# A two-layer hybrid block on one core: which raw buffer a condition block takes, and at which ticks condition sums are made

## The chip, the cores and the metric

The kernel runs on 1 core of one Trainium2 chip. The metric is the device time of one execution in microseconds (us); it was 1853.11 us as the median of three runs (1845.4 to 1854.9).

The engines of the core, by the names of the profile: PE is the tensor engine (matmuls; PEld its weight loads), DVE the vector engine (VectorE), ACT the scalar engine, POOL the GpSimd engine, SP the engine that issues most transfers (DMAs). Each engine takes its own instructions in program order; semaphores order them across engines.

## The reference

Two layers of a transformer-like block on 512 tokens of width 1024. What matters here is the conditioning vector c: per layer it gives six vectors of 1024 numbers, by a matrix of 1024 x 6144.

```python
c_act = jax.nn.silu(c)
for l in range(DEPTH):                       # DEPTH = 2
    x = hybrid_layer(x, c_act, ...)

def hybrid_layer(x, c_act, ...):
    mod = c_act @ w_ada + b_ada
    shift1, scale1, gate1, shift2, scale2, gate2 = jnp.split(mod, 6, axis=-1)
    h = modulate(rms_norm(x, norm1_g), shift1, scale1)
    ...                                      # projections, three branches, gates
    mixed = jnp.sum(gates * y_br, axis=2) @ w_o
    x = x + gate1[:, None, :] * mixed
    h2 = modulate(rms_norm(x, norm2_g), shift2, scale2)
    u, g = jnp.split(h2 @ w_up, 2, axis=-1)
    u = causal_dwconv(u, w_conv, b_conv)
    y = (jax.nn.silu(u) * g) @ w_down        # D_FF = 2816
    x = x + gate2[:, None, :] * y
    return x
```

## The kernel before

**Weight units.** All large weights are cut into units of 128 x 1024 floats (512 KB), eight blocks of 128 x 128, in the order in which they are used. A unit passes four stations. `dma_to` loads it into one of six raw buffers (`wr`, `NR = 6`; L180, issued by SP). `prep_hi` rounds it on ACT to the matmul's format (`wh`, L194). `prep_lo` takes the remainder on DVE (`wl`, L203); after that the raw buffer is no longer needed. Then PE uses both: `mm3` makes three matmuls for each block (L321 to L323: high times high, high times low, low times high). `wh` and `wl` have five buffers each, and the preparation runs up to four units ahead of use (`depth`).

**Condition blocks.** The six vectors of a layer are 48 columns of 128 numbers, called by section 0 to 5 (shift1, scale1, gate1, shift2, scale2, gate2), eight blocks each. A block is 128 x 1024 floats of `wada`. `ada_dma` loads the next block into a raw buffer of the same six (tile `ar`, L225, issued by SP), one at a time. `ada_sum` multiplies it on DVE by the broadcast condition and sums each row (L230, 128 x 1024 in one instruction, and a read of the accumulator). `ada_step` does the sum of the block that is loaded and at once issues the load of the next. `ada_need(l, sec)` repeats steps until a section is complete. Sections 0 and 1 of layer 0 are made apart at the start; the other 80 blocks go through this queue, in order, layer 0 first.

**Which raw buffer.** The planner `buffer` runs while the program is built. `held[b]` is the number of the unit with which buffer b comes free; a buffer may be taken when `held[b] < state["lo"]`, where `state["lo"]` counts the remainders made so far. Of those it takes the one with the lowest number, that is, the one longest free. A loaded condition block has the number 1 << 30; its sum sets it back.

**When.** The program is written by hand in one order (`manual_schedule`), and each engine takes its part of it. `tick` is called at fixed places between matmuls. It moves small attention work on, runs what is pending (`flush`, such as the evacuation of a finished bank), and calls `ada_step` at every other tick, or at every tick while `ada_fast` is set; `ada_on` switches this on and off. It is on in the mix (gates, branches and the output projection), in the first part of the feed-forward stage and in the down projection.

**Around the change.** The stages of a layer: projections and branches; the mix, whose last tiles `mixed` are split into `mxh` and `mxl` (L562, L563) for the output projection with `w_o`; the feed-forward stage, at first by column blocks, with up to six units loaded ahead, then in three groups of seven half-size products (`ff_group`), for which raw weights are added up in place by accumulating loads from POOL (L186); then the down projection. This has 22 row blocks (kc) for each of 8 column blocks (j). Columns 0 to 2 are computed together, kc by kc, with a tick after every second kc. Columns 3 to 7 follow one by one, with a tick after every fourth kc; in layer 0 column 7 is computed last in two halves, with the next norm (L376 is its first matmul) between. `dn_evac` adds a finished column to x (L1023) and, in layer 0, its square to `acc` (L360, L361). In the down projection `ada_on` and `ada_fast` are set at kc = 8 of the first three columns.

Of the kernel before, what the change touches and what calls it, by code (L numbers as in the profile page):

```python
# [91 lines left out]
def tile_hybrid_layers(ctx: ExitStack, tc: tile.TileContext, xT, cvec, wall, wada, par, a2, cst, tabs, out):  # L92
# [15 lines left out]
    def slot(nm, dt=F32):  # L108
        return slots.tile([128, S], dt, tag="slot", name=nm)

    def bm(nm="bm"):
        return psm.tile([128, S], F32, tag="m", name=nm)
# [32 lines left out]
    state = {"prep": 0, "lo": 0, "dma": 0}  # L145
# [14 lines left out]
    held = [-1] * NR  # L160
# [54 lines left out]
    ada_buf = [0]  # L215
# [10 lines left out]
            ada_raw.append((l, b, post, r))  # L226

    def ada_sum(l, b, r):
        held[ada_buf[0]] = -1
        V.scalar_tensor_tensor(out=r, in0=r, scalar=1.0, in1=cact, op0=ALU.mult, op1=ALU.mult,  # L230
                               accum_out=mod[l][:, b:b + 1])

    def ada_step():
        if ada_raw:
            l, b, post, r = ada_raw.pop(0)
            ada_sum(l, b, r)
            if post:
                post()
        ada_dma()

    def ada_need(l, sec):
        while any(j[:2] <= (l, sec * 8 + 7) for j in ada_raw + ada_jobs):
            ada_step()
# [30 lines left out]
    def flush():  # L274
        while pend:
            pend.pop(0)()

    def advance(kind):
        for g in list(active):
            t = g[1]  # L280
            if g[2] or t[0] != kind:
                continue
            if kind == "p" and live[0] + t[1] > NA:
                return
            if len(t) > 2 and not all(t[2]()):
                return
            g[2] = True
            g[1] = next(g[0], None)
            if g[1] is None:
                active.remove(g)  # L290

    def tick(n=1, fl=True):
        for g in active:
            g[2] = False
        if cool[0] > 0:
            cool[0] -= 1
        if queue and len(active) < 8 and cool[0] == 0:
            it, cool[0] = queue.pop(0)
            active.append([it, next(it), False])
        advance("e")  # L300
        if fl:
            flush()
        advance("p")
        if ada_on[0] and (ada_fast[0] or tickcount[0] % 2 == 1):
            ada_step()
        tickcount[0] += 1
        if DBG:
            print("T", tickcount[0], len(active), len(queue), live[0], cur[0], [g[0].__name__ for g in active])

    tickcount = [0]  # L310
    cool = [0]
    ada_on = [True]
    ada_fast = [False]

    def drain():
        flush()
        while active or queue:
            tick(1)

    def mm3(o, wh, wl, ah, al, first, last):  # L320
        T.matmul(o, lhsT=wh, rhs=ah, start=first, stop=False)  # L321
        T.matmul(o, lhsT=wh, rhs=al, start=False, stop=False)  # L322
        T.matmul(o, lhsT=wl, rhs=ah, start=False, stop=last)  # L323
# [16 lines left out]
    def col_block(act, evac, half=True, ticks=1):  # L340
        ahead()
        wh, wl = unit()
        o = bm()
        for kc in range(KD):
            sl = slice(kc * 128, kc * 128 + 128)
            mm3(o, wh[:, sl], wl[:, sl], act[kc][0], act[kc][1], kc == 0, kc == KD - 1)
            if kc == 3:
                tick(ticks)
        pend.append(lambda: evac(o))
        tick(ticks, False)  # L350
# [204 lines left out]
    def split(src, nm, scale=None):  # L555
        hi = slot(nm + "h", F32R)
        lo = slot(nm + "l", F32R)
        if scale is None:
            A.copy(hi, src)
            V.tensor_tensor(lo, src, hi.bitcast(F32), op=ALU.subtract)  # L560
        else:
            A.activation(hi, src, AF.Copy, scale=scale)  # L562
            V.scalar_tensor_tensor(out=lo, in0=src, scalar=scale, in1=hi.bitcast(F32), op0=ALU.mult, op1=ALU.subtract)  # L563
        return hi, lo

    def layer(l, nm, h):
# [520 lines left out]
        def act_to(n):  # L1087
            for k in range(min(n, KFF)):
                if acts[k] is None:
                    acts[k] = split(act[k], "fa")  # L1090
                    act[k] = None
# [165 lines left out]
        while ada_raw:  # L1257
            i, b, post, r = ada_raw.pop(0)
            ada_sum(i, b, r)
            if post:  # L1260
                post()
# [20 lines left out]
        def wd(j, kc):  # L1282
            f = DNI[j, kc]
            if f // 8 not in got:
                ahead()
                got[f // 8] = unit()
            sl = slice((f % 8) * 128, (f % 8) * 128 + 128)
            return got[f // 8][0][:, sl], got[f // 8][1][:, sl]
# [4 lines left out]
        def dn_evac(j, o):  # L1293
            upd5(j, o)
            if last:
                store(j)
            else:
                square_acc(j, acc3)

        xl = list(range(KD))  # L1300
        act_to(4)
        far[0] = 4
        o2 = [bm() for _ in range(NI)]
        for kc in range(KFF):
            for j in range(NI):
                wh, wl = wd(j, kc)
                mm3(o2[j], wh, wl, acts[kc][0], acts[kc][1], kc == 0, kc == KFF - 1)
            for _ in range(2):
                if rest:
                    rest.pop(0)()  # L1310
            act_to(kc + 4)
            if xl and kc >= 4:
                k = xl.pop(0)
                x[k] = slot("x")
                Q.dma_start(out=x[k], in_=xm[l, k])
            if kc == 8:
                ada_on[0] = True
                ada_fast[0] = True
                far[0] = 1
            if kc % 2:  # L1320
                tick()
        ada_need(l, 5)
        for j in range(NI):
            pend.append(lambda j=j: dn_evac(j, o2[j]))
        for j in range(NI, KD if last else KD - 1):
            o = bm()
            for kc in range(KFF):
                wh, wl = wd(j, kc)
                mm3(o, wh, wl, acts[kc][0], acts[kc][1], kc == 0, kc == KFF - 1)
                if kc % 4 == 3:  # L1330
                    tick()

            pend.append(lambda j=j, o=o: dn_evac(j, o))
        flush()
        ada_fast[0] = False
        if last:
            return None, None
        ada_need(l + 1, 0)
# [5 lines left out]
    with tc.manual_schedule():  # L1344
# [39 lines left out]
        for l in range(L):  # L1384
            nm, h = layer(l, nm, h)
# [171 lines left out]
```

## Time and profile before

| | |
|---|---|
| three runs | 1845.4, 1853.11, 1854.9 us; median 1853.11 |
| the profiled execution | 1846.68 us, its span (first to last instruction) 1844.5 us |
| mean granted TensorE clock | 0.985 |
| ACT busy | 743.5 us (40%) |
| POOL busy | 147.7 us (8%) |
| read from HBM, written | 250.00 MB, 8.40 MB |
| condition blocks loaded by L225 | 80 of 512 KB, first sum at 292.6 us, last at 1262.0 us |
| share of the chain that ended last: PE, DVE, DMA | 72%, 12%, 8% |

How to read the views. A row of groups has line, engine, operation, output <- inputs by the program's tile names, the shape and the count. A row of waits has the waiting engine, tile and line, then the releasing engine, tile and line, then us in total, how many times, and the longest. A row of windows has the window, then for PE, PEld, DVE, ACT and POOL the busy us with the count of instructions, then the granted clock, the share of the 16 DMA engines that was busy, and GB/s. A row of the timeline has start, duration, engine, line, operation; in brackets the idle time of that engine before it and what ended it; SPq is SP's queue of transfers. A row of a tile has minimum, median and maximum duration in ns, then first and last start. The busy time of a matmul overlaps with the next, so a busy PE is not PE at its peak; the distance of starts tells more.

### The profile page before, as it was taken

The page shows a single profiled execution, that of the slowest core. Times are in us where ns is not written, and L with a number is a line of the kernel's source. Part 1 is how long each engine was busy: PE and PEld are TensorE (multiplying, and loading weights), DVE is VectorE, ACT ScalarE, POOL GpSimd, SP SyncE. Part 2 cuts the span into 40 slices and gives each one's busy share as a digit, 9 for nine tenths or more (in the row PEclk, how much of TensorE's full clock was granted, in tenths as well). Part 3 has the DMA queues.
Part 4 walks back from the last instruction along what each step waited for, and adds up shares of the span by engine and source line. Part 5 has one row for each costly group of instructions (what it writes and reads, how often), then busy time and mean ns, then how long its engine had stood idle before and what let it go on. Part 6 is the DMA issues. An engine that isn't in the chain of part 4 may idle for free.

```text
span 1844.5 us, 24358 instructions
## 1 busy us (share of the span) xinstructions
PE 1784.8 (97%) x9601; PEld 1527.7 (83%) x9601; DVE 1085.7 (59%) x1639; ACT 743.5 (40%) x1233; POOL 147.7 (8%) x191
## 2 busy tenths in 40 slices
PE   8999999999899979999869999999999999999999
PEld 6888788888788869998668888788888898899887
DVE  7767654555566766685445667554434466566831
ACT  4664433422234335562115744333323234455520
POOL 3211100000010011100000101000000000111000
PEclk9999999999999989999979999999999999999999
DMA  9331232454462468854453322314242333488421
GB/s 359 126 130 58 74 99 83 146 181 177 168 223 97 161 184 215 212 200 166 177 194 110 108 92 69 104 69 149 92 147 93 122 108 92 121 210 217 160 99 50
DMA packets 78510, 259.99 MB, mean 141 GB/s; under 512 B 9096, under 2 KB 9522, under 8 KB 78396
## 3 DMA queue, kind: packets, MB, share of 16 engines
q1 hardware_dynamic: 68748, 224.86, 34.9%
q0 software_dynamic: 9648, 33.58, 8.6%
q8 instruction: 75, 1.23, 0.3%
q14 instruction: 39, 0.32, 0.0%
HBM read 250.00 MB, written 8.40 MB: 140 GB/s over the span
## 4 chain that ended last, share of the span: by engine, by line
PE 72%; DVE 12%; DMA 8%; ACT 4%; issue 3%; SPq 0%; POOL 0%; DVEq 0%; ACTq 0%; POOLq 0%
PE bm L321 13%; PE bm L322 13%; PE bm L323 13%; DMA ar<-wada 6%; PE bm L460 4%; PE ga L460 4%; PE bm L628 3%; PE bm L629 3%; PE bm L630 3%; PE bm L1159 3%; PE bm L1162 3%; PE bm L1161 3%; DMA wr<-wall 3%; DVE ar L230 2%; DVE wl L203 2%
## 5 line engine op out<-in xcount | busy, mean ns | idle before, releaser
L203 DVE TENSOR_TENSOR wl<-wr,wh 128x1024 fp32r<-128x1024 f32 x338 | 412.4, 1223 | 291.2 <-ACT wh L194 288.1
L194 ACT CAST wh<-wr 128x1024 fp32r<-128x1024 f32 x338 | 351.5, 1047 | 363.2 <-DMA wr<-wall 210.6
L321 PE MATMUL bm<-hhi,wh 128*128 128x512 f32 x912 | 366.1, 401 | 0.0
L323 PE MATMUL bm<-hhi,wl 128*128 128x512 f32 x912 | 355.7, 390 | 0.0
L322 PE MATMUL bm<-hlo,wh 128*128 128x512 f32 x912 | 355.5, 390 | 0.0
L321 PEld LDWEIGHTS bm<-hhi,wh 128*128 128x128 f32 x912 | 171.3, 188 | 37.1 <-issue 2.8
L323 PEld LDWEIGHTS bm<-hhi,wl 128*128 128x128 f32 x912 | 171.2, 188 | 37.1
L322 PEld LDWEIGHTS bm<-hlo,wh 128*128 128x128 f32 x912 | 171.5, 188 | 35.8 <-issue 1.4
L323 PE MATMUL bm<-fah,wl 128*128 128x512 f32 (+1 forms) x374 | 145.9, 390 | 17.2 <-DVE wl L203 17.2
L230 DVE SCALAR_TENSOR_TENSOR ar<-ar,cact 128x1024 f32<-128x1024 f32 x80 | 97.8, 1222 | 91.9 <-DMA ar<-wada 91.8
L321 PE MATMUL bm<-fah,wh 128*128 128x512 f32 (+1 forms) x374 | 145.7, 390 | 1.1 <-ACT wh L194 1.1
L322 PE MATMUL bm<-fal,wh 128*128 128x512 f32 (+1 forms) x374 | 144.9, 387 | 0.0
L323 PEld LDWEIGHTS bm<-fah,wl 128*128 128x128 f32 x374 | 74.5, 199 | 31.9 <-DVE wl L203 18.8
L628 PE MATMUL bm<-wh,hhi 128*128 128x512 f32 (+1 forms) x256 | 96.1, 376 | 0.0
L629 PE MATMUL bm<-wl,hhi 128*128 128x512 f32 (+1 forms) x256 | 93.5, 365 | 0.0
L630 PE MATMUL bm<-wh,hlo 128*128 128x512 f32 (+1 forms) x256 | 93.3, 365 | 0.0
L321 PEld LDWEIGHTS bm<-fah,wh 128*128 128x128 f32 x374 | 74.6, 200 | 14.3 <-ACT wh L194 1.4
L322 PEld LDWEIGHTS bm<-fal,wh 128*128 128x128 f32 x374 | 74.5, 199 | 13.1
L186 POOL DMA_DIRECT2D wr<-wall x48 | 41.7, 987 | 377.3 <-DVE wl L203 215.2
L321 PE MATMUL bm<-mxh,wh 128*128 128x256 f32 (+1 forms) x176 | 59.8, 340 | 8.0 <-ACT mxh L562 8.0
L322 PE MATMUL bm<-mxl,wh 128*128 128x256 f32 (+1 forms) x176 | 59.6, 338 | 0.0
L323 PE MATMUL bm<-mxh,wl 128*128 128x256 f32 (+1 forms) x176 | 59.1, 336 | 0.0
(288 smaller groups left out, 3368.5 us busy)
## 6 DMA issues: line engine op xcount, KB each, us to landing
wr<-wall SPq DMA_DIRECT2D x302, 512.0 KB, 4.3
ar<-wada SPq DMA_DIRECT2D x80, 512.0 KB, 3.5
wr<-wall POOLq DMA_DIRECT2D x48, 512.0 KB, 9.2
ad<-wada SPq DMA_DIRECT2D x32, 256.0 KB, 6.4
x<-xT SPq DMA_DIRECT2D x16, 256.0 KB, 4.5
x<-xm SPq DMA_DIRECT2D x16, 256.0 KB, 5.9
xm<-x POOLq DMA_DIRECT2D x10, 256.0 KB, 2.5
cumb<-cumd POOLq DMA_DIRECT2D x8, 256.0 KB, 4.8
```

Source lines behind the costliest of these rows:

```text
L194: A.copy(hi, raw[plan[i][1]])
L203: V.tensor_tensor(lo, raw[plan[i][1]], hi.bitcast(F32), op=ALU.subtract)
L230: V.scalar_tensor_tensor(out=r, in0=r, scalar=1.0, in1=cact, op0=ALU.mult, op1=ALU.mult, accum_out=mod[l][:, b:b + 1])
L321: T.matmul(o, lhsT=wh, rhs=ah, start=first, stop=False)
L322: T.matmul(o, lhsT=wh, rhs=al, start=False, stop=False)
L323: T.matmul(o, lhsT=wl, rhs=ah, start=False, stop=last)
L460: T.matmul(banks[f % GB][:, ts], lhsT=got[f // 8][wi][:, (f % 8) * 128:(f % 8) * 128 + 128], rhs=h[kc][hi][:, ts], start=kc == 0 and hf != ...
L628: T.matmul(o, lhsT=h[k][0][:, bs], rhs=wh[:, ws], start=k == 0, stop=False)
L629: T.matmul(o, lhsT=h[k][0][:, bs], rhs=wl[:, ws], start=False, stop=False)
L630: T.matmul(o, lhsT=h[k][1][:, bs], rhs=wh[:, ws], start=False, stop=k == KD - 1)
L1159: T.matmul(o, lhsT=wh[:, sl], rhs=ah, start=first and i == 0 and k == 0, stop=False, skip_group_check=True)
L1161: T.matmul(o, lhsT=wh[:, sl], rhs=al, start=False, stop=False, skip_group_check=True)
```

## The change

There are two edits. First, a raw buffer whose sum has been made gets the number `state["lo"] - 1` in place of -1: it still counts as free, but as freed just now, so the planner takes a buffer that has been free for longer. Second, `ada_fast` is removed, so sums are made at every other tick everywhere; in the down projection they begin after the first three columns, ticks in columns 3 and on come after every third kc in place of every fourth, and the call that needs section 5 stands ahead of the stage. Blocks left over stay in the queue for the next layer's mix.

```diff
     def ada_sum(l, b, r):
-        held[ada_buf[0]] = -1
+        held[ada_buf[0]] = state["lo"] - 1
...
-        if ada_on[0] and (ada_fast[0] or tickcount[0] % 2 == 1):
+        if ada_on[0] and tickcount[0] % 2 == 1:
             ada_step()
...
-    ada_fast = [False]
...
         xl = list(range(KD))
+        ada_need(l, 5)
         act_to(4)
...
             if kc == 8:
-                ada_on[0] = True
-                ada_fast[0] = True
                 far[0] = 1
             if kc % 2:
                 tick()
-        ada_need(l, 5)
+        ada_on[0] = True
         for j in range(NI):
             pend.append(lambda j=j: dn_evac(j, o2[j]))
...
-                if kc % 4 == 3:
+                if kc % 3 == 2:
                     tick()
...
         flush()
-        ada_fast[0] = False
```

From L314 up to the head of the down projection, lines of the changed kernel have a number lower by one (L1023 is L1022, L1010 is L1009, L361 is L360). Three places show how instructions move; the buffers that are taken do not show in such rows.

On DVE in the down projection of layer 0, from the update of column 2 on (L1023 or L1022 adds a column to x, L361 or L360 its square; L230 is a sum, L203 the remainder of a weight unit; L252 adds the bias of a section). Before:

```order
670 L1023 SCALAR_TENSOR_TENSOR x<-bm,mod_87,x 128x512
671 L361 TENSOR_TENSOR acc<-acc,sq 128x512
672 L230 SCALAR_TENSOR_TENSOR ar,mod_88<-ar,cact 128x1024
673 L252 TENSOR_TENSOR mod_88<-mod_88,par_86 128x8
674 L203 TENSOR_TENSOR wl<-wr,wh 128x1024
675 L230 SCALAR_TENSOR_TENSOR ar,mod_88<-ar,cact 128x1024 x2
676 L203 TENSOR_TENSOR wl<-wr,wh 128x1024
677 L230 SCALAR_TENSOR_TENSOR ar,mod_88<-ar,cact 128x1024 x2
678 L203 TENSOR_TENSOR wl<-wr,wh 128x1024
679 L1023 SCALAR_TENSOR_TENSOR x<-bm,mod_87,x 128x512
```

And of the change, from a remainder to the update of column 4:

```order
666 L203 TENSOR_TENSOR wl<-wr,wh 128x1024
667 L230 SCALAR_TENSOR_TENSOR ar,mod_88<-ar,cact 128x1024 x2
668 L203 TENSOR_TENSOR wl<-wr,wh 128x1024
669 L1022 SCALAR_TENSOR_TENSOR x<-bm,mod_87,x 128x512
670 L360 TENSOR_TENSOR acc<-acc,sq 128x512
671 L230 SCALAR_TENSOR_TENSOR ar,mod_88<-ar,cact 128x1024
672 L203 TENSOR_TENSOR wl<-wr,wh 128x1024
673 L230 SCALAR_TENSOR_TENSOR ar,mod_88<-ar,cact 128x1024
674 L203 TENSOR_TENSOR wl<-wr,wh 128x1024
675 L230 SCALAR_TENSOR_TENSOR ar,mod_88<-ar,cact 128x1024
676 L203 TENSOR_TENSOR wl<-wr,wh 128x1024
677 L1022 SCALAR_TENSOR_TENSOR x<-bm,mod_87,x 128x512
```

Two sums stood for each remainder at most places; now it is one, or two at some. The stage has 13 sums in place of 26.

On SP at the same stage (L225 loads a condition block, L180 a weight unit). Before:

```order
130 L225 DMA ar<-wada 128x1024 x4
131 L180 DMA wr<-wall 128x1024
132 L225 DMA ar<-wada 128x1024
133 L180 DMA wr<-wall 128x1024
134 L225 DMA ar<-wada 128x1024 x2
135 L180 DMA wr<-wall 128x1024
136 L225 DMA ar<-wada 128x1024 x2
```

And of the change:

```order
128 L180 DMA wr<-wall 128x1024 x2
129 L225 DMA ar<-wada 128x1024
130 L180 DMA wr<-wall 128x1024
131 L225 DMA ar<-wada 128x1024
132 L180 DMA wr<-wall 128x1024
133 L225 DMA ar<-wada 128x1024 x2
134 L180 DMA wr<-wall 128x1024
```

Where one or two (once four) condition loads stood ahead of each weight load, mostly one does.

On DVE in the mix of layer 1 (L1009 and L1010, or L1008 and L1009, are the gated sums of the branches). Before:

```order
1003 L1009 SCALAR_TENSOR_TENSOR mg<-mg,bm 128x512
1004 L1010 TENSOR_TENSOR mix<-mix,mg 128x512
1005 L1009 SCALAR_TENSOR_TENSOR mg<-mg,bm 128x512
1006 L1010 TENSOR_TENSOR mix<-mix,mg 128x512
1007 L203 TENSOR_TENSOR wl<-wr,wh 128x1024 x3
```

And of the change:

```order
1000 L1008 SCALAR_TENSOR_TENSOR mg<-mg,bm 128x512
1001 L1009 TENSOR_TENSOR mix<-mix,mg 128x512
1002 L1008 SCALAR_TENSOR_TENSOR mg<-mg,bm 128x512
1003 L1009 TENSOR_TENSOR mix<-mix,mg 128x512
1004 L230 SCALAR_TENSOR_TENSOR ar,mod_88<-ar,cact 128x1024
1005 L203 TENSOR_TENSOR wl<-wr,wh 128x1024
1006 L230 SCALAR_TENSOR_TENSOR ar,mod_88<-ar,cact 128x1024
1007 L203 TENSOR_TENSOR wl<-wr,wh 128x1024 x2
```

Here sums now stand between the remainders: the mix of layer 1 has 18 sums in place of 5.

## The prediction

> **What bounds the kernel now.** I read the page first, then the waits of the tensor engine, the matmuls of equal stages in both layers, windows of 20 us, and last the timeline of the places found.
>
> ```profile
> PE 1784.8 (97%) x9601; PEld 1527.7 (83%) x9601; DVE 1085.7 (59%) x1639; ACT 743.5 (40%) x1233; POOL 147.7 (8%) x191
> ```
>
> The tensor engine carries the kernel, so the time is that of the matmul stream plus the gaps in it. Its waits, over the whole span:
>
> ```profile
> PE bm L323 <- DVE wl L203: 17.2, 5, 4.4
> PE ba L1159 <- ACT wh L194: 9.1, 1, 9.1
> PE nrm L376 <- DVE acc L361: 8.2, 2, 5.8
> PE bm L321 <- ACT mxh L562: 8.0, 2, 7.3
> PE bm L1159 <- ACT uu L1176: 3.3, 1, 3.3
> ```
>
> They wait for prepared weights (wl, wh), for mixed activations (mxh) and for the sum of squares (acc). Layer 1 runs the same stages almost without condition sums, so it shows what layer 0 loses. First the output projection (mxh), layer 0 and layer 1, then the down projection (fah):
>
> ```profile
> L321 PE MATMUL bm<-mxh,wh x88: 277/283/795, 497.6 to 554.3; 128*128 128x256 f32 x48, 128*128 128x512 f32 x40
> L321 PE MATMUL bm<-mxh,wh x88: 278/283/389, 1443.2 to 1488.2; 128*128 128x256 f32 x48, 128*128 128x512 f32 x40
> L321 PE MATMUL bm<-fah,wh x198: 278/389/628, 805.1 to 963.0; 128*128 128x512 f32 x154, 128*128 128x256 f32 x44
> L321 PE MATMUL bm<-fah,wh x176: 389/389/396, 1720.4 to 1839.5; 128*128 128x512 f32 x176
> ```
>
> - Output projection: 56.7 us against 45.0, a loss of **11.7**.
> - From it to the down projection (the feed-forward stage): 805.1 - 554.3 = 250.8 against 1720.4 - 1488.2 = 232.2, a loss of **18.6**.
> - Down projection: layer 1 starts 3 x 176 matmuls of 512 columns in 119.1 us, 0.227 us each. Layer 0 has 3 x 154 of them (104.8 us) and 132 of 256 columns. In layer 1's output projection 120 wide ones leave 45.0 - 27.2 = 17.8 us for 144 narrow ones, 0.124 each, so 16.3 us here. That makes 121.1 us against 157.9, a loss of **36.8**.
>
> Together 67.1 us. The windows say the same: x90 is a full stage of wide matmuls, and the granted clock falls where there are gaps.
>
> ```profile
> 420.00:440.00 20.00, 20.00 (x90) 16.56 (x89) 10.69 (x15) 3.38 (x4) 0.00 (x0) 1.00 0.69 241
> 500.00:520.00 20.00, 11.96 (x39) 8.32 (x38) 13.06 (x18) 5.41 (x7) 0.60 (x1) 0.74 0.52 188
> 680.00:700.00 20.00, 14.66 (x103) 14.37 (x104) 10.88 (x12) 8.54 (x11) 4.35 (x5) 0.75 0.77 189
> 900.00:920.00 20.00, 15.85 (x65) 12.34 (x64) 8.64 (x13) 3.78 (x4) 0.54 (x1) 0.96 0.48 171
> 920.00:940.00 20.00, 10.60 (x48) 9.68 (x48) 9.01 (x15) 2.61 (x3) 0.54 (x1) 0.72 0.50 170
> 1340.00:1360.00 20.00, 20.00 (x90) 16.57 (x89) 8.42 (x10) 5.86 (x7) 0.00 (x0) 1.00 0.57 197
> ```
>
> The cause is a closed loop. All condition blocks of a stretch go through one raw buffer, so a block's load waits for the sum before it, and VectorE then waits for that load:
>
> ```profile
> wr<-wall SPq DMA_DIRECT2D x302, 512.0 KB, 4.3
> L230 DVE SCALAR_TENSOR_TENSOR ar<-ar,cact x80: 1210/1221/1227, 292.6 to 1262.0; 128x1024 f32<-128x1024 f32 x80
> L230 DVE DVE_READ_ACCUMULATOR ar<-ar,cact x80: 78/83/88, 293.8 to 1263.2; 128x1 f32 x80
>   DMA ar<-wada: 91.8, 38
> DMA to landing us min/median/max: 3.3/3.5/6.0
> 905.53 5.09 SPq L225 DMA_DIRECT2D ar<-wada  x2
> 909.03 1.23 DVE L230 SCALAR_TENSOR_TENSOR ar<-ar,cact 128x1024 f32<-128x1024 f32 x1 [3.52 <-DMA ar<-wada]
> 910.18 1.22 DVE L203 TENSOR_TENSOR wl<-wr,wh 128x1024 fp32r<-128x1024 f32 x1
> 910.71 0.38 SPq L180 DMA_DIRECT2D wr<-wall  x1
> 913.88 1.23 DVE L230 SCALAR_TENSOR_TENSOR ar<-ar,cact 128x1024 f32<-128x1024 f32 x1 [2.48 <-DMA ar<-wada]
> 915.14 1.05 ACT L194 CAST wh<-wr 128x1024 fp32r<-128x1024 f32 x1 [9.04 <-DMA wr<-wall]
> 915.14 5.14 SPq L225 DMA_DIRECT2D ar<-wada  x2
> ```
>
> One turn is 3.5 us to land and 1.3 us of sum, 4.8. From 905.53 to 915.14 two turns pass, 9.6 us, and SP, which takes its queue in order, lets one weight transfer through. A weight unit is 24 matmuls, 5.45 us of tensor work, so the tensor engine uses up its lead of prepared units and then starves.
>
> **The change, part by part.**
>
> *Down projection.* Besides sums and weight remainders VectorE has one update and one square sum here for each column block:
>
> ```profile
> 876.50 0.75 DVE L1023 SCALAR_TENSOR_TENSOR x<-bm,mod,x 128x512 f32<-128x512 f32 x1
> 878.00 0.69 DVE L361 TENSOR_TENSOR acc<-acc,sq 128x512 f32<-128x512 f32 x1 [0.76 <-ACT sq L360]
> ```
>
> A column block (66 wide matmuls, 15.0 us) now has 7 ticks and 3.5 sums, where it had 5 ticks and 5 sums; the stage makes 13 sums where it made 26. Even with the loop closed, 3.5 x 4.8 = 16.8 us per block would fall 1.8 us behind, 7 us over four blocks, and VectorE enters with some four prepared units (wl has five buffers), 4 x 5.45 = 22 us. And the loop opens: the freed buffer now counts as the youngest, six buffers go round, and a load waits for a step that stands five to seven VectorE steps (weight remainders and sums) before its own use, where it was one or two. VectorE's load per block is 2.75 x 1.22 + 3.5 x 1.31 (with the accumulator's read) + 1.44 = 9.4 of 15.0 us. Transfers are 6.25 x 0.524 MB in 15.0 us, 218 GB/s; the row at 900 moved 171 at a share of 0.48, so about 356 would be all of it. Both fit. I take the whole 36.8; if the wait for the sum of squares (longest 5.8) stayed, 31.0.
>
> *End of the mix, layer 0.* The last mixed tile is behind two sums that wait for loads, and a cast on ACT is behind a weight transfer that stands behind such a load:
>
> ```profile
> 497.44 0.38 SPq L180 DMA_DIRECT2D wr<-wall  x1
> 500.62 1.23 DVE L230 SCALAR_TENSOR_TENSOR ar<-ar,cact 128x1024 f32<-128x1024 f32 x1 [2.50 <-DMA ar<-wada]
> 501.83 1.04 ACT L194 CAST wh<-wr 128x1024 fp32r<-128x1024 f32 x1 [5.18 <-DMA wr<-wall]
> 505.83 1.23 DVE L230 SCALAR_TENSOR_TENSOR ar<-ar,cact 128x1024 f32<-128x1024 f32 x1 [1.70 <-DMA ar<-wada]
> 506.98 0.68 DVE L1009 SCALAR_TENSOR_TENSOR mg<-mg,bm 128x512 f32<-128x512 f32 x1
> 508.43 0.63 ACT L562 ACTIVATE mxh<-mix 128x512 fp32r<-128x512 f32 x1 [4.96 <-DVE mix L1010]
> ```
>
> Without the waits at least 2.50 + 1.70 = 4.2 us go, and with the cast's 5.18 more than the 7.3 that the tensor engine waits. The range is 4.2 to 11.7; I take 11.7, as layer 1's row has no such wait.
>
> *Start of the feed-forward groups, layer 0.* Loads run far ahead here and leave one buffer free, so most sums still return to the buffer just freed; by the buffer rule only the last three find another. The first two rows keep their times:
>
> ```profile
> 670.41 1.22 DVE L230 SCALAR_TENSOR_TENSOR ar<-ar,cact 128x1024 f32<-128x1024 f32 x1
> 675.30 1.22 DVE L230 SCALAR_TENSOR_TENSOR ar<-ar,cact 128x1024 f32<-128x1024 f32 x1 [2.52 <-DMA ar<-wada]
> 680.48 1.23 DVE L230 SCALAR_TENSOR_TENSOR ar<-ar,cact 128x1024 f32<-128x1024 f32 x1 [3.54 <-DMA ar<-wada]
> 683.79 1.03 ACT L194 CAST wh<-wr 128x1024 fp32r<-128x1024 f32 x1
> ```
>
> The load of the sum at 675.30 can now go before the sum at 670.41, so that sum loses its wait of 2.52 and stands at 672.8. The last load goes at 671.7, the end of the sum at 670.41, lands 3.5 us later, and its sum starts at 675.2, 5.2 us earlier than 680.48. The cast at 683.79 that ends the wait of 9.1 us follows it. I take 5.2; the ends are 0 (the accumulating loads bind anyway) and 18.6.
>
> The row at 680 has a clock of 0.75, 10 us at half rate, at most 5 us lost. The Trainium skill, "TensorE: Matmul & The Clock Gate", Part 1, says the clock halves after about one idle window of 3.4 us and that the windows run freely. By it the gap of about 4 us that I leave here still pays for a slow stretch, as in my sum; were it shorter than a window, the sum would be up to 2.5 us less. The trace agrees that gaps and clock go together.
>
> *Layer 1's mix* takes the 13 sums: 13 x 1.31 = 17.0 us of VectorE. What hides them is the same stretch of layer 0, which already makes such sums and keeps x90 (row at 420), and VectorE's idle time there (8.42 busy of 20 at 1340). If that cover failed, 17.0 us would come back. The conditions are used first after the mix. Moving the call for section 5 and the switch costs nothing: those sums are done by then.
>
> **Sum.** 36.8 + 11.7 + 5.2 = 53.7 us. From the profiled execution, 1846.7 us (span 1844.5 and 2.2 around it), that gives 1793.0. The three runs stand from 1.3 below to 8.2 above that execution, with the median 6.4 above; I add half of this: **1796 us**.
>
> **Rivals.**
>
> 1. *Only the slower pace counts.* Where the buffer rule brings nothing at the other two places (a load queued behind weight transfers lands no earlier), 36.8 goes: 1809.9. For it: nine of the fifteen sums of the feed-forward stretch keep their buffer.
> 2. *The down projection stays starved* by another term of its VectorE order (block updates wait for the tensor engine, sums behind them), while the other two places gain 16.9: 1829.8. Against it: layer 1's stage, with the same updates, has no gap.
> 3. *Transfers bind.* What is won on VectorE is lost again as weight transfers share bandwidth with sums: 1846.7. Against it: 218 of some 356 GB/s.
> 4. *All of the feed-forward loss goes too:* 1846.7 - 67.1 = 1779.6.
> 5. *Slower: weights starve in the shared rotation.* Until now weights had five buffers of their own, nine or more VectorE steps ahead; now a weight load is released five steps ahead. If VectorE does these back to back, that is 5 x 1.25 = 6.2 us, against 4.3 to land and 1.05 of cast, 5.35. At a landing time of 6.0 (the longest of the condition blocks) each unit would be 0.8 us late; over the 88 units that share buffers with sums (42 + 14 + 11 in layer 0, 21 in layer 1, by the program's order) that is 70 us: 1793 + 70 = 1863. It decides for slower from a landing time of 5.9. Against it: VectorE runs at the tensor engine's pace, where five steps take near three units, 15 us. The Trainium skill, "Trainium Kernel Development and Optimization", Key Constraints, says that DMAs of all queues interleave on the same 16 engines, which speaks for this one, since more loads will be under way together; the trace has weight loads at 4.3, issued just behind a condition block, against 3.5.
>
> **How the numbers follow.** The forecast gets 0.70, the rivals in order 0.13, 0.05, 0.05, 0.04 and 0.03. About 0.5% is what a measurement can tell from no change here: faster 0.92, same 0.05, slower 0.03. The forecast's bounds are 67.1 and 35.2 us of gain (4.2 + 0 + 31.0), 1780 to 1811, without and with 6.4 for the median up to 1818. The range 1778 to 1818 holds the forecast and rivals 1 and 4, 0.87.
>
> **What would show it.** In the changed profile: the down projection of layer 0 with 90 matmuls per 20 us up to its last block and no wait of bm for wl; VectorE's idle time before L230 far below 91.8 us; the output projection of layer 0 near 45 us; one wait of about 4 us left at the start of the feed-forward groups; layer 1's mix still at x90. It would be wrong if sums there still wait for loads with their data issued early, or if casts in layer 1's mix begin to wait for weights.

## The result and the profile after

The changed kernel takes **1799.34 us** (median of four runs, 1797.49 to 1804.63), the kernel before 1852.37 (four runs). The ratio is 0.9724, 95% interval 0.9691 to 0.9758. The profiled execution took 1799.28 us, its span is 1797.2, and the mean granted clock 0.994 (before: 0.985).

From the page of the changed kernel, the busy times; from its waits, the tensor engine's, over the whole span:

```profile
PE 1771.0 (99%) x9601; PEld 1518.8 (85%) x9601; DVE 1084.3 (60%) x1639; ACT 741.2 (41%) x1233; POOL 147.1 (8%) x191
```
```profile
PE bm L1158 <- ACT uu L1175: 6.4, 4, 3.4
PE bm L1158 <- DVE fu L1067: 3.0, 1, 3.0
PE nrm L375 <- DVE acc L360: 2.8, 1, 2.8
...
PE ba L1158 <- ACT wh L194: 1.8, 1, 1.8
```

The waits of bm for wl (17.2 us) and for mxh (8.0) are gone. That for acc is the one at 12 us, at the kernel's start; the 5.8 of the down projection is gone too. Of the waits that are left, only those of L1158, the feed-forward groups, lie in the stages compared here. The stages of layer 0, as rows of the tiles mxh and fah:

```profile
L320 PE MATMUL bm<-mxh,wh x88: 278/283/389, 497.3 to 542.3; 128*128 128x256 f32 x48, 128*128 128x512 f32 x40
L320 PE MATMUL bm<-fah,wh x198: 278/389/396, 794.7 to 915.8; 128*128 128x512 f32 x154, 128*128 128x256 f32 x44
```

- Output projection: 45.0 us (56.7 before).
- Feed-forward stage: 794.7 - 542.3 = **252.4** (250.8 before): it gained nothing.
- Down projection: 121.1 us (157.9 before).

36.8 + 11.7 - 1.6 = 46.9 of the 47.4 us between the two profiled executions. Windows of the changed kernel, for the end of the mix, the feed-forward groups, the down projection and layer 1's mix:

```profile
500.00:520.00 20.00, 20.00 (x90) 16.55 (x89) 15.20 (x21) 6.20 (x8) 1.69 (x3) 1.00 0.73 248
680.00:700.00 20.00, 16.57 (x118) 16.36 (x117) 8.37 (x9) 8.20 (x9) 1.94 (x3) 0.83 1.00 245
860.00:880.00 20.00, 20.00 (x90) 16.55 (x89) 12.56 (x19) 4.74 (x5) 0.54 (x1) 1.00 0.72 252
1300.00:1320.00 20.00, 20.00 (x90) 16.58 (x89) 10.90 (x15) 4.32 (x5) 0.00 (x0) 1.00 0.80 285
```

Both repaired places and layer 1's mix, with its extra sums, stand at x90 and full clock; only the feed-forward row does not. How VectorE waits for condition blocks, from the tile ar:

```profile
L230 DVE SCALAR_TENSOR_TENSOR ar<-ar,cact x80: 1215/1218/1226, 292.3 to 1306.6; 128x1024 f32<-128x1024 f32 x80
  DMA ar<-wada: 8.5, 4
DMA to landing us min/median/max: 3.4/4.2/6.6
```

The loads land later than before (4.2 against 3.5), and yet 91.8 us of waiting have become 8.5: they are issued early.

### The profile page after: what moved, and what is told of

It reads as the page before. It is cut to its first block, busy times and chain, and to the rows that moved or that the text cites. A ratio compares the mean times of both kernels' runs of the same rounds, so it can differ in the third digit from the quotient of the medians.

```text
span 1797.2 us, 24309 instructions
## 1 busy us (share of the span) xinstructions
PE 1771.0 (99%) x9601; PEld 1518.8 (85%) x9601; DVE 1084.3 (60%) x1639; ACT 741.2 (41%) x1233; POOL 147.1 (8%) x191
## 3 DMA queue, kind: packets, MB, share of 16 engines
q1 hardware_dynamic: 68748, 224.86, 36.8%
## 4 chain that ended last, share of the span: by engine, by line
PE 82%; DVE 9%; DMA 3%; ACT 3%; issue 2%; SPq 0%; POOL 0%; ACTq 0%; DVEq 0%; POOLq 0%
PE bm L320 17%; PE bm L322 17%; PE bm L321 17%; PE bm L459 4%; PE ga L459 4%; PE bm L627 3%; PE bm L628 3%; PE bm L629 3%; PE bm L1158 3%; PE bm L1160 2%; PE bm L1161 2%; DMA wr<-wall 2%; ACT wh L194 1%; PE ba L1161 1%; PE ba L1160 1%
## 5 line engine op out<-in xcount | busy, mean ns | idle before, releaser
L203 DVE TENSOR_TENSOR wl<-wr,wh 128x1024 fp32r<-128x1024 f32 x338 | 412.3, 1223 | 293.1 <-ACT wh L194 292.1
L322 PEld LDWEIGHTS bm<-hhi,wl 128*128 128x128 f32 x912 | 171.2, 188 | 36.8
L320 PE MATMUL bm<-fah,wh 128*128 128x512 f32 (+1 forms) x374 | 141.0, 377 | 0.0
L321 PE MATMUL bm<-fal,wh 128*128 128x512 f32 (+1 forms) x374 | 140.8, 377 | 0.0
L322 PE MATMUL bm<-fah,wl 128*128 128x512 f32 (+1 forms) x374 | 140.8, 377 | 0.0
L230 DVE SCALAR_TENSOR_TENSOR ar<-ar,cact 128x1024 f32<-128x1024 f32 x80 | 97.4, 1219 | 8.5 <-DMA ar<-wada 8.5
L322 PEld LDWEIGHTS bm<-fah,wl 128*128 128x128 f32 x374 | 70.4, 188 | 13.0
L320 PEld LDWEIGHTS bm<-fah,wh 128*128 128x128 f32 x374 | 70.4, 188 | 12.8
L321 PEld LDWEIGHTS bm<-fal,wh 128*128 128x128 f32 x374 | 70.4, 188 | 12.7
L1022 DVE SCALAR_TENSOR_TENSOR x<-bm,mod,x 128x512 f32<-128x512 f32 (+1 forms) x39 | 25.3, 654 | 80.6 <-PE bm L322 80.5
L985 ACT ACTIVATE mg<-bm,der 128x512 f32<-128x512 f32 x48 | 32.9, 685 | 73.7 <-PE bm L322 73.7
L1158 PE MATMUL bm<-tbh,wh 128*128 128x256 f32 x192 | 56.0, 292 | 6.4 <-ACT uu L1175 6.4
```

The costliest lines, as they stand in the source:

```text
L203: V.tensor_tensor(lo, raw[plan[i][1]], hi.bitcast(F32), op=ALU.subtract)
L1158: T.matmul(o, lhsT=wh[:, sl], rhs=ah, start=first and i == 0 and k == 0, stop=False, skip_group_check=True)
```

## Experiments

Ratios are to runs of the kernel before on the same chip, with 95% intervals. Stages are those of layer 0 in the profiled execution, by the rows used above, so each is a single reading; waits are VectorE's for condition blocks. (The expectations count the feed-forward stage from a matmul 0.2 us later.)

| kernel | output proj. | feed-forward | down proj. | waits | median us | ratio |
|---|---|---|---|---|---|---|
| before | 56.7 | 250.8 | 157.9 | 91.8 | 1852.37 | |
| after | 45.0 | 252.4 | 121.1 | 8.5 | 1799.34 | 0.9724 (0.9691 to 0.9758) |
| c_after | 45.0 | 250.9 | 121.1 | 6.3 | 1798.78 | 0.9716 (0.9692 to 0.9740) |
| e1_rule | 45.0 | 254.8 | 121.1 | 16.3 | 1801.77 | 0.9713 (0.9693 to 0.9733) |
| e2_pace | 56.3 | 254.3 | 123.6 | 68.3 | 1819.01 | 0.9811 (0.9785 to 0.9836) |
| e3_noff | 45.0 | 233.3 | 121.1 | 10.3 | **1781.35** | 0.9608 (0.9588 to 0.9628) |
| e4_keep2 | 45.0 | 245.3 | 121.1 | 0.8 | 1794.28 | 0.9682 (0.9657 to 0.9708) |
| e5_dve | 45.0 | 241.7 | 121.1 | 10.3 | 1788.55 | 0.9666 (0.9638 to 0.9694) |
| e6_dma | 45.0 | 233.9 | 121.1 | 9.1 | 1783.37 | 0.9632 (0.9611 to 0.9653) |
| e7_noff_closed | 58.8 | 239.8 | 160.4 | 90.6 | 1835.53 | 0.9906 (0.9874 to 0.9939) |
| e8_dve_half | 45.0 | 233.7 | 121.1 | 8.8 | 1784.39 | 0.9642 (0.9615 to 0.9668) |
| e9_dve_double | 45.0 | 255.6 | 121.1 | 9.6 | 1803.01 | 0.9745 (0.9723 to 0.9768) |

### Each of the two edits alone

e1_rule is the kernel before with the buffer rule only:

```diff
     def ada_sum(l, b, r):
-        held[ada_buf[0]] = -1
+        held[ada_buf[0]] = state["lo"] - 1
```

> The buffer rule alone, with the pace of before (sums at every tick in the down projection, 26 of them). My theory: the closed loop is the cause, so opening it is enough: output projection of layer 0 at 45 us (was 57), down projection at 121 to 126 us (was 158; a column block holds 5 sums, 11.5 of 15.0 us on VectorE), waits of L230 for its loads below 15 us (was 92), feed-forward stage as in the changed kernel, about 252 us. Median 1797 to 1806 us. Rival (the pace is needed, VectorE or the transfers bind at two sums for each weight unit): down projection stays above 135 us, median above 1812 us.

e2_pace is the changed kernel with that line put back, so the pace only:

```diff
     def ada_sum(l, b, r):
-        held[ada_buf[0]] = state["lo"] - 1
+        held[ada_buf[0]] = -1
```

> The slower pace alone, the buffer freed as before, so that each load waits for the sum before it. My theory: the down projection is covered all the same (3.5 sums x 4.8 us fall 1.8 us behind in each 15.0 us block, 7 us in all, against a lead of 22 us): 121 to 124 us; the end of the mix keeps its loss, output projection 57 us; feed-forward stage 250 us as before; waits of L230 70 to 90 us. Median 1812 to 1818 us. Rival (the buffer rule is what opened the down projection): it stays above 135 us, and the median above 1825 us.

The same two stages, in e1_rule and then in e2_pace:

```profile
L321 PE MATMUL bm<-mxh,wh x88: 278/284/390, 497.9 to 542.9; 128*128 128x256 f32 x48, 128*128 128x512 f32 x40
L321 PE MATMUL bm<-fah,wh x198: 277/389/396, 797.7 to 918.8; 128*128 128x512 f32 x154, 128*128 128x256 f32 x44
```
```profile
L320 PE MATMUL bm<-mxh,wh x88: 278/284/795, 497.6 to 553.9; 128*128 128x256 f32 x48, 128*128 128x512 f32 x40
L320 PE MATMUL bm<-fah,wh x198: 278/389/397, 808.2 to 931.8; 128*128 128x512 f32 x154, 128*128 128x256 f32 x44
```

The buffer rule alone frees both stages, though 26 sums still go through the down projection at five to a column block. The pace alone frees the down projection to within 2.5 us, and leaves the output projection as it was. So the gains overlap in one stage, and only the rule repairs the other. The ratios of e1_rule and of the changed kernel cannot be told apart. Some details missed: VectorE's waits in e1_rule are 16.3 us (below 15 expected), and e2_pace has a feed-forward stage of 254.3 us (250), waits of 68.3 (70 to 90) and a median of 1819.01, just above its 1812 to 1818.

### The feed-forward stretch without condition sums

e3_noff switches the sums off for the column blocks of the feed-forward stage and makes up for them in the down projection, 21 there and the rest in layer 1's mix:

```diff
+        ada_on[0] = False
+        while ada_raw:
+            i, b, post, r = ada_raw.pop(0)
+            ada_sum(i, b, r)
+            if post:
+                post()
         fb = head_group(l, 3, nm2, h2, True)
...
-                if kc % 3 == 2:
+                if kc % 2:
                     tick()
```

> The changed kernel without condition sums in the feed-forward stage of layer 0 (the block under way is summed ahead of it); in columns 3 on of the down projection ticks come after every second kc, which gives 21 sums there, and the mix of layer 1 takes 24. Theory A (the loss left in the feed-forward stage, 252 us against 232 in layer 1, comes from the sums in it, which put VectorE behind and end in a closed loop): stage 232 to 236 us, waits of bm for uu and fu gone, down projection still near 121 us, median 1779 to 1785 us. Theory B (the loss comes from the accumulating loads and would be there without the sums): stage above 245 us, median above 1792 us.

The stage falls to 233.3 us, layer 1's 232.2 but for 1.1, and the other two stages of the table stay as they were. By its median this is the fastest kernel of the study, and its interval lies below that of the changed kernel. With the condition sums the loss in that stretch is gone in this execution; e7_noff_closed below, also without sums there, had 239.8 us, so not every execution has all of it.

e7_noff_closed is e3_noff with the old buffer rule:

```diff
-        held[ada_buf[0]] = state["lo"] - 1
+        held[ada_buf[0]] = -1
```

> The kernel without sums in the feed-forward stage and with 21 sums in the down projection, but with the buffer freed as before the change (each load waits for the sum before it). My theory of loop and lead: 5.5 sums x 4.8 us = 26.4 us in each block of 15.0 us, 11.4 behind per block, 46 over four blocks, less a lead of 22: down projection about 145 us (138 to 155), output projection 57 us, feed-forward stage near 233 us; median 1808 to 1830 us. Rival (the loop only matters with sums at every tick): down projection below 128 us, median below 1798 us.

The tensor engine's waits of e7_noff_closed in the down projection, and two of its windows:

```profile
PE bm L322 <- DVE wl L203: 17.9, 6, 4.5
PE nrm L375 <- DVE acc L360: 6.4, 1, 6.4
PE bm L320 <- ACT wh L194: 2.7, 3, 1.3
```
```profile
900.00:920.00 20.00, 14.82 (x58) 11.75 (x58) 8.04 (x15) 2.09 (x2) 0.00 (x0) 0.85 0.46 158
920.00:940.00 20.00, 10.43 (x53) 9.61 (x52) 8.41 (x12) 3.08 (x4) 0.54 (x1) 0.74 0.50 170
```

With the loop closed, 5.5 sums to a column block starve the stage again: 160.4 us. Its waits are 27.0 us; of the other 12.3 of the 39.3 above 121.1, about 9 are the clock (0.85 and 0.74 in these rows), by busy time times missing clock over rows of 10 us, an estimate; my expectation had left the clock out, and the rest was not traced. The output projection (58.8 for 57), the feed-forward stage (239.8 for 233) and the median (1835.53 for at most 1830) came out above the expectation too. The same pace with the rule costs nothing in the down projection (e3_noff, 121.1).

### What in the sums costs the feed-forward stage its time

c_after is the changed kernel once more, unaltered.

> The changed kernel once more, unaltered, to see how far its feed-forward stage varies. If the small gaps of its second and third group (some 5 us) belong to the kernel, they are there again and the stage is 251 to 255 us; if they were chance, it is 246 to 249 us. Median 1797 to 1803 us.

e4_keep2 keeps two buffers free for condition blocks where one was kept, so that the loop opens in this stretch as well; weight loads far ahead have one buffer less for it:

```diff
-            b = buffer(endv[i], soft, 1 if ada_on[0] and ada_jobs else 0)
+            b = buffer(endv[i], soft, 2 if ada_on[0] and ada_jobs else 0)
```

> The changed kernel with two raw buffers in place of one kept free from loads far ahead, so that in the feed-forward stage a condition load finds another buffer than the one just summed. Theory A1 (there the closed loop costs the time): waits of L230 near 0, the tensor engine's waits in the stage (about 13 us in gaps and 7 us by the clock) fall to half or less, stage 240 to 246 us, median 1787 to 1793 us. Theory A2 (VectorE's work costs it: remainder 1.2, sum 1.3, evacuation 1.1 and the sums of the half-size products 1.9 us, 5.5 of 5.45 us for each unit): waits of L230 gone, but the stage stays above 248 us and the median within 4 us of 1799 us.

e5_dve is e3_noff with VectorE's work alone: 14 operations of a sum's size on data that is always there, written to a tile that nothing reads. Here and in e6_dma, `extra` is set in the column blocks of layer 0 that follow the first three; the lines that set it, and those of e3_noff, are left out.

```diff
+        if extra[0] and tickcount[0] % 2 == 1:
+            scr = uu_p.tile([128, 2 * S], F32, tag="uu", name="scr")
+            jnk = sm_p.tile([128, 2], F32, tag="part", bufs=4, name="jnk")
+            V.scalar_tensor_tensor(out=scr, in0=cact, scalar=1.0, in1=cact, op0=ALU.mult, op1=ALU.mult,
+                                   accum_out=jnk[:, 0:1])
```

> The kernel without sums in the feed-forward stage (233 us there), with 14 instructions of a sum's size put back at the same ticks of that stage; they multiply the broadcast condition by itself into a tile of their own, so they need no load and no raw buffer. Theory A2 (VectorE's work makes what the kernel with two free buffers still lost, 245 us against 233): stage 240 to 246 us, median 1788 to 1795 us. Theory A3 (the extra transfers make it): stage within 3 us of 233, median within 4 us of 1781 us.

e6_dma is e3_noff with the loads alone, 14 by the trace, at the same ticks, one buffer kept and nothing summed:

```diff
+        if extra[0] and tickcount[0] % 2 == 1:
+            if xbuf:
+                held[xbuf.pop(0)] = state["lo"] - 1
+            n = buffer(1 << 30, True)
+            if n is not None:
+                r = wr_p.tile([128, D], F32, tag=f"wr{n}", name="ax")
+                Q.dma_start(out=r, in_=wada[tickcount[0] % 48])
+                xbuf.append(n)
```

> The kernel without sums in the feed-forward stage, with 15 loads of a condition block put back at the same ticks into the one buffer kept free, with nothing computed from them. Theory A3 (the transfers cost it): stage 240 to 246 us, median 1788 to 1795 us. Theory A2 (VectorE's work costs it): stage within 3 us of 233, median within 4 us of 1781 us.

Against e3_noff the stage grows by 0.6 us for the loads alone, 8.4 for VectorE's work alone, 12.0 for whole sums with the loop open, and 17.6 and 19.1 with one buffer (c_after, after). e5_dve and e6_dma came out as theory A2 had it. e4_keep2 has the stage of A1 and waits of 0.8, but a median just above (1794.28), and its interval overlaps those of e5_dve and c_after, so what the closed loop adds is not shown by it. c_after (250.7 as the expectation counts) lies between its two cases; waits in the second and third group are there again.

Two more kernels vary the work: e8_dve_half has 7 such operations, e9_dve_double 28.

```diff
-        if extra[0] and tickcount[0] % 2 == 1:
+        if extra[0] and tickcount[0] % 4 == 1:
```

> The kernel of e5 with an idle sum-sized VectorE operation at every fourth tick of the eight column blocks, 7 in place of 14 (9.1 us in place of 18.3). In e5 14 of them made the feed-forward stage of layer 0 8.4 us longer (233.1 to 241.5) and put the third accumulating load 4.8 us later. Theory (VectorE has some 10 to 13 us to spare before those loads, and only what goes beyond that comes back as time): the 7 fit, the stage stays at 233 to 235, the median at 1781 to 1784 us. Rival (each operation costs the same 0.6 us, by pushing something that is always late): the stage about 237, the median about 1785.

```diff
-        if extra[0] and tickcount[0] % 2 == 1:
+        if extra[0]:
```

> The kernel of e5 with two idle sum-sized VectorE operations where that had one, 28 in place of 14 (36.6 us in place of 18.3). Theory (what goes beyond VectorE's spare time comes back one to one): another 18.3 us, third accumulating load at about 138 us from the end of the output projection (119.3 in e5), the stage at about 260, the median at about 1807 us. Rival (0.6 us for each operation): the stage about 250, the median about 1796.

The window from 640 us in e3_noff (no such operation) and in e5_dve (14):

```profile
640.00:660.00 20.00, 20.00 (x110) 17.44 (x109) 9.11 (x11) 6.88 (x9) 3.49 (x4) 1.00 0.21 32
```
```profile
640.00:660.00 20.00, 20.00 (x103) 17.12 (x102) 18.23 (x26) 8.12 (x11) 0.86 (x1) 1.00 0.21 68
```

In the timeline, the first issue of three accumulating loads in a row on POOL, in e3_noff, e8_dve_half (7), e5_dve and e9_dve_double (28):

```profile
657.26 2.63 POOL L186 DMA_DIRECT2D wr<-wall  x3 [9.83 <-DVE wl L203]
```
```profile
657.84 2.63 POOL L186 DMA_DIRECT2D wr<-wall  x3 [6.75 <-DVE wl L203]
```
```profile
663.83 2.63 POOL L186 DMA_DIRECT2D wr<-wall  x3 [4.66 <-DVE wl L203]
```
```profile
677.42 2.63 POOL L186 DMA_DIRECT2D wr<-wall  x3 [5.79 <-DVE wl L203]
```

Counted from the end of the output projection these issues stand at 114.8, 114.7, 119.5 and 135.5 us, and they wait for a remainder (wl) each time. The stage is 0, 0.4, 8.4 and 22.3 us longer. VectorE is half idle in that window without the work (9.11 of 20) and nearly full with 14 operations (18.23). How much work was added, the timeline of e9_dve_double tells:

```profile
639.84 1.22 DVE L309 SCALAR_TENSOR_TENSOR scr<-cact 128x1024 f32<-128x1024 f32 x1
...
640.98 1.22 DVE L309 SCALAR_TENSOR_TENSOR scr<-cact 128x1024 f32<-128x1024 f32 x1
```

One follows another after 1.14 us, so the durations of the rows overlap, and the 7, 14 and 28 operations are 8.0, 16.0 and 32.0 us of VectorE, not the 9.1, 18.3 and 36.6 of the expectations. (The pages agree: VectorE is busy for 1084.0, 1091.4, 1099.5 and 1115.4 us in the four kernels.) Of the 16.0 us that e9_dve_double has beyond e5_dve, 16.0 come back as lateness of these loads.

The stage as a whole hides this, because its second part varies by itself. So here it is cut at the first product of the tile tbh, in the first feed-forward group; all sums and all added operations lie ahead of it. The rows for before, after and c_after:

```profile
L1159 PE MATMUL bm<-tbh,wh x96: 278/283/415, 705.6 to 804.7; 128*128 128x256 f32 x96
```
```profile
L1158 PE MATMUL bm<-tbh,wh x96: 280/283/581, 690.4 to 794.4; 128*128 128x256 f32 x96
```
```profile
L1158 PE MATMUL bm<-tbh,wh x96: 278/283/582, 686.7 to 792.7; 128*128 128x256 f32 x96
```

| kernel | work in the first part | first part | second part |
|---|---|---|---|
| e3_noff | none | 135.4 | 97.9 |
| e7_noff_closed | none, old buffer rule | 135.4 | 104.4 |
| e6_dma | 14 loads | 135.4 | 98.5 |
| e8_dve_half | 7 operations | 135.4 | 98.3 |
| e5_dve | 14 operations | 138.7 | 103.0 |
| e9_dve_double | 28 operations | 154.8 | 100.8 |
| e4_keep2 | sums, two buffers kept | 144.1 | 101.2 |
| c_after | sums, the change | 144.5 | 106.4 |
| after | sums, the change | 148.1 | 104.3 |
| e1_rule | sums, buffer rule alone | 149.1 | 105.7 |
| e2_pace | sums, old buffer rule | 151.1 | 103.2 |
| before | sums, old buffer rule | 151.3 | 99.5 |

In the first part the theory holds: the first 8.0 us of work cost nothing, the next 8.0 cost 3.3, and the last 16.0 cost 16.1 (clock included). So VectorE has 8.0 + 4.7 = 12.7 us to spare there, an estimate, and what goes beyond comes back one to one; a fixed price for each operation, the rival, does not fit. In e9_dve_double this does not all go through the accumulating loads: waits for wh, wl and fu of 5.5 us come already in the column blocks, ahead of the groups. Whole sums with two buffers kept cost 5.4 us more than 14 bare operations; which of load, buffer or wait makes these was not separated. The loop's share is open too: c_after is only 0.4 above e4_keep2, after 4.0.

The second part takes 97.9 to 106.4 us, with no sum in it, and differs by 3.7 between before and e2_pace, which have the same code in this stage, by 2.1 between after and c_after, which are one program, and by 6.5 between e3_noff and e7_noff_closed. What makes it vary was not found. So differences of a few us between whole stages, as between e4_keep2 and c_after, show nothing. The median of e8_dve_half (1784.39) lies between the two expectations and cannot tell them apart; the first part can. The stage of e9_dve_double (255.6) lies between its two as well.

## Why the prediction was right, and which step failed

- **Down projection, 36.8:** right, 157.9 to 121.1 as the sum had it, the wait for acc included. e2_pace bears out the step on the closed loop: at 3.5 sums to a block it costs 2.5 us, 2.2 of them one wait for acc and none for weights, so the lead of prepared units covers it. e7_noff_closed shows the loop as the cause: at 5.5 sums it takes the stage back to 160.4.
- **End of the mix, 11.7:** right, 45.0 us as in layer 1, and by the buffer rule alone (45.0 in e1_rule, 56.3 in e2_pace).
- **Layer 1's mix, nothing:** right; x90 at 1300 with VectorE at 10.90 of 20.
- **Rivals:** pace alone (1809.9) falls with e1_rule, where the buffer rule repairs the output projection by itself; only in the feed-forward stage did the rule bring nothing, as that rival had it; a down projection starved by its own updates, and transfers that bind, fall with its 121.1 us at 252 GB/s; that all of the feed-forward loss goes falls with 252.4. Weights that starve in the shared rotation do not occur. In the down projection they did land later, by the rows of L180 from 805 to 915 us, before and after:

```profile
DMA to landing us min/median/max: 3.5/4.3/5.5
```
```profile
DMA to landing us min/median/max: 3.4/5.1/6.1
```

The median stayed under the 5.9 at which that rival decides, and the tensor engine did not wait for wl or wh there.

- **Feed-forward stage, 5.2: the step that failed; the stage gained nothing (1.6 us longer).** The step read: "the last load goes at 671.7 ... its sum starts at 675.2, 5.2 us earlier than 680.48. The cast at 683.79 that ends the wait of 9.1 us follows it." In the changed kernel:

```profile
655.59 1.23 DVE L230 SCALAR_TENSOR_TENSOR ar<-ar,cact 128x1024 f32<-128x1024 f32 x1 [2.59 <-DMA ar<-wada]
...
659.56 0.55 PE L1158 MATMUL bm<-hhi,wh 128*128 128x256 f32 x1 [3.00 <-DVE fu L1067]
...
665.46 1.23 DVE L230 SCALAR_TENSOR_TENSOR ar<-ar,cact 128x1024 f32<-128x1024 f32 x1 [0.78 <-DMA ar<-wada]
...
668.77 1.03 ACT L194 CAST wh<-wr 128x1024 fp32r<-128x1024 f32 x1
...
669.85 0.38 PE L1158 MATMUL ba<-tah,wh 128*128 128x256 f32 x1 [1.77 <-ACT wh L194]
...
688.86 1.04 ACT L194 CAST wh<-wr 128x1024 fp32r<-128x1024 f32 x1 [2.95 <-DMA wr<-wall]
689.81 0.58 ACT L1175 COPY uu<-bm 128x512 f32<-128x512 f32 x1
...
690.44 0.58 PE L1158 MATMUL bm<-tbh,wh 128*128 128x256 f32 x1 [3.43 <-ACT uu L1175]
```

From the end of the output projection the last sum stands at 123.2 us (126.2 before) and the cast at 126.5 (129.5): both 3.0 earlier, and the cast did follow. The tensor engine's wait for it fell from 9.1 to 1.8. But 3.0 us of waiting now come ahead of it, where a bank's evacuation on VectorE (fu) stands behind a sum that waits for its load. And 6.4 (3.3 before) come behind it, where an evacuation on ACT (uu) stands behind casts of accumulated weights, themselves late. In the whole stage these waits went from 13.9 us (9.1 + 3.3 + 0.8 + 0.7) to 12.0 (6.4 + 3.0 + 1.8 + 0.8), 1.9 us less. The clock took that back. The rows of 10 us with the largest part of it, tensor engine alone (busy, clock, DMA share, GB/s), before and then after:

```profile
680.00:690.00 10.00, 4.66 (x20) 0.50 0.55 139
700.00:710.00 10.00, 6.66 (x45) 0.86 0.95 260
```
```profile
660.00:670.00 10.00, 8.23 (x49) 0.73 0.65 163
670.00:680.00 10.00, 9.24 (x63) 0.83 0.84 195
...
690.00:700.00 10.00, 9.56 (x59) 0.70 0.94 235
```

Before, the long gap fell in large part into its own time at half clock. Busy time by missing clock is 4.66 x 0.50 + 6.66 x 0.14 = 3.3 us in these rows and 0.3 in the others. After, shorter gaps leave the slow stretches to running work: 8.23 x 0.27 + 9.24 x 0.17 + 9.56 x 0.30 = 6.7 us, and 0.8 in the others. The 3.9 more and the 1.9 less make 2.0, an estimate; 1.6 was measured.

Two things in the step were wrong. The smaller one is the start: it lets the sum at 670.41 (116.1 us from the end of the output projection) keep its time, but in the changed kernel that sum came at 118.5, behind waits of 2.02 and 2.59 for loads, and the two behind it followed at 120.8 and 123.2. c_after, the same program, shows the larger one. There that sum is at 116.3, and all goes as the step had it:

```profile
663.19 1.23 DVE L230 SCALAR_TENSOR_TENSOR ar<-ar,cact 128x1024 f32<-128x1024 f32 x1 [0.81 <-DMA ar<-wada]
...
666.50 1.03 ACT L194 CAST wh<-wr 128x1024 fp32r<-128x1024 f32 x1
...
667.59 0.39 PE L1158 MATMUL ba<-tah,wh 128*128 128x256 f32 x1 [3.79 <-ACT wh L194]
```

The last sum stands at 121.0 us, 5.2 earlier than before, the cast at 124.3, also 5.2 earlier, and one wait of 3.8 is left. The first part of the stage is 6.8 us shorter (144.5 for 151.3; 3.2 in after). Yet the stage takes 250.9, because its second part is 6.9 longer (106.4 for 99.5; 4.8 in after), with waits for uu in the second and third group where before had none. So the step that failed is to count time won at the cast as time of the stage. Why the second part took it back stays open: it varies without a sum in it, and e2_pace, whose sums in this stage are as late as before, has 103.2. That late accumulating loads carry the loss on is likely from the casts that wait for them, but no run shows it. That the first part pays for VectorE's mere work is shown (e5_dve, e9_dve_double); the step had priced only the wait of one sum.

- **The offset to the median:** I added 3.0 us, about half of 6.4. The changed kernel's median equals its profiled execution, so no offset was needed. That execution lies 6.3 us above the 1793.0 of the sum, and the feed-forward term alone is 6.8 too good (5.2 + 1.6); the offset hid half of that. That the forecast of 1796 came within 3.3 us is in this part luck.

## What to carry to other kernels

A free buffer handed out again at once ties each load to the consumer just before it; handing out the one longest free opens that loop, and cost nothing here even though loads then landed later. Where two edits repair the same stall, run each alone: their gains overlapped almost wholly in one stage. Before pricing a wait by the one instruction that ends it, look at how full the engine is in the windows ahead, and do not count a wait that gets shorter as time won before the end of the stage shows it. In a stretch where an engine is full, what helped here was to move the work to a stage with idle time, as e3_noff does. When a stage varies by itself, cut it where the work under test ends.

## What the runs showed of the hardware

Half clock came after gaps that I had thought short. Stretches cut at the changes of the clock, tensor engine alone, in the changed kernel:

```profile
655.00:658.40 3.40, 1.56 (x14) 1.00 0.35 142
658.40:665.30 6.90, 5.74 (x27) 0.51 0.48 153
665.30:672.00 6.70, 4.17 (x32) 1.00 0.83 230
672.00:675.50 3.50, 3.50 (x19) 0.52 0.72 112
```

A wait of 3.00 us (up to 659.56) was followed, from 658.4 on, by 6.9 us at half clock, and two waits of 1.77 and 0.76 us with a little work between them by another 3.5. The Trainium skill, "TensorE: Matmul & The Clock Gate", Part 1, puts the threshold at one idle window of about 3.4 us. Neither the one wait nor the two were that long, so here the trace does not bear out that a window must be idle throughout; why they were enough was not tried. The prediction had weighed a gap too short to bring a slow stretch; these were shorter than the 4 us left in its sum, and had theirs. Length alone does not decide it either. In e5_dve a wait of 3.16 us, longer than the first of these, was followed by none:

```profile
683.00 0.39 PE L1164 MATMUL bm<-tbh,wh 128*128 128x256 f32 x1 [3.16 <-ACT uu L1181]
```
```profile
680.00:700.00 20.00, 17.00 (x141) 17.00 (x142) 11.72 (x13) 11.72 (x15) 1.73 (x2) 1.00 0.82 228
```

On VectorE, in e9_dve_double, instructions of a sum's size that stand back to back start 1.14 us apart (639.84, 640.98), though each row says 1.22.
